# Load order, a second broadcast bank and a residual kept in DRAM in a two-layer mLSTM and attention trunk

## The chip, the cores and the metric

The kernel runs on one core of a Trainium2 chip. The metric is the device time of one execution in microseconds (us), as the median of several runs. One core has a matrix engine (PE), which multiplies, a vector engine (DVE), an activation engine (ACT), GpSimd (POOL) and a sync engine (SP), which here issues nearly all transfers between DRAM and the on-chip memory. Each engine takes its instructions strictly in the order of the program and meets the others through semaphores.

## The reference, cut to what matters

```python
def rmsnorm(x, g):
    return x * lax.rsqrt(jnp.mean(x * x, axis=-1, keepdims=True) + EPS) * g

def swiglu(h, w_gate, w_up, w_down):
    return (jax.nn.silu(h @ w_gate) * (h @ w_up)) @ w_down

h = x                                       # (1, 1024, 1024) float32, d_ff = 2816
for l in range(2):
    if l == 1:
        kv = rmsnorm(h, kv_norm_g) @ w_kv   # shared keys and values, 16 heads of 64
    hn = rmsnorm(h, norm_mix_g[l])
    if l == 0:
        h = h + mlstm_mixer(hn, ...)        # 8 heads, chunks of 64
    else:
        h = h + chunked_relpos_attention(hn, w_q, rel_table, w_o, k_sh, v_sh)
    h = h + swiglu(rmsnorm(h, norm_ffn_g[l]), w_gate[l], w_up[l], w_down[l])
return rmsnorm(h, final_norm_g)
```

## The kernel before, in words

All activations lie transposed: eight tiles of 128 features by 1024 tokens. A float32 product is made of three products of a short float type: ACT casts an operand to its high half (L174, L177, L965), DVE or GpSimd subtracts to get the low half (L175, L178, L967), and PE runs high times high, low times high and high times low. PE can start on an operand when its high half is there, and needs the low half one matmul later.

Both feed-forward blocks use seven block products in place of eight, with sums of blocks on either side. The gate and up projections, `gate_up`, go through 22 units of weight columns, n = 0 to 21, each with seven products, c = 0 to 6, of 12 matmuls into the PSUM tiles `a`, `b`, `c`, `d` (L989). `prepare(n, c)` makes the weight operand `wc` of product (n, c); units 0 and 1 run interleaved, since their first four products need only the left half of the tokens. During these first products the norm's scale is finished: `finish_a` sums squares over the features on PE (`f_ps`), DVE works out the inverse root (`f_y`), and `finish_b` spreads it with PE over all partitions into a PSUM bank (`f_pb`, four matmuls for each half of the tokens), from which ACT copies it to `f_rbc` (L341). Both halves use the same bank in turn.

The down projection, `down`, runs products i = 0 to 6 (operands b11, b21, t4, t3, t2, n1, b22, kept in DRAM by `gate_up`), each for u = 0 to 3, with 33 matmuls a product (PE line L1261, 11 blocks of the hidden features times three). `fetch(i, k)` loads block k of operand i into a tile of the `hr` pool (six tiles, 256 KB each) and splits it into `hc`; `wload(u, i, j)` loads a block of down weights (`wd`, 704 KB); `prepare(i, u)` splits such a block into `wc`, for which there are two tiles. For i = 0 the weights are loaded a second time, into three tiles of the `hr` pool (`wd1first`, L1157). The kept rows of the residual, `h[e]` (`hr` from `hd`, 512 KB), are loaded at L1238 and L1247, and DVE adds each product to them in `settle` (L1200); ACT copies the product of i = 0 to `v` (L1198).

At the end of layer 0 each row of the result is split into `xb{e}` high and low (`final`). The attention layer uses these halves, and at its end `out_a` puts the residual together again as high plus low with GpSimd (L1467). At that place PE runs the last attention products and the first half of the output projection (`oa_p`), whose operands `os0` to `os3` DVE splits (L175).

The final norm: `scale_out` sums squares over features on PE (`fin_ps`), works out the root on DVE (`fin_v` to `fin_y`), spreads it (`fin_pb`), and multiplies the rows on DVE (L1187) and GpSimd (L1185) before they are stored. It is called for the left half of the tokens after product (4, 3), and for two quarters after (6, 3, 0) and (6, 3, 1); in the last layer product 6 runs as two passes of 256 tokens.

SP issues all loads of these parts in one order. There are eight semaphores for its transfers, taken in turn, so an issue also waits for the eighth one before it to land.

Of the kernel before, what the change touches and what calls it, by code (L numbers as in the profile page):

```python
# [8 lines left out]
F32 = mybir.dt.float32  # L9
# [6 lines left out]
P = 128  # L16
T = 1024
# [23 lines left out]
def tile_trunk(  # L41
# [54 lines left out]
    def mxt(name):  # L96
        return pools["mx"].tile([P, HT], F32, tag="mx", name=name)
# [82 lines left out]
    def split(src, name, scale=None, pool="core"):  # L180
        hi = full(pool, f"{name}h", F32R)
        lo = full(pool, f"{name}l", F32R)
        split_into(hi, lo, src, scale)
        return hi, lo
# [103 lines left out]
    class Stats:  # L288
# [37 lines left out]
        def finish_b(self, r_tok, r_bc, cols=slice(0, T), pin=False):  # L326
            t0, nt = cols.start // P, (cols.stop - cols.start) // P
            for i0 in range(0, nt, 4):
                n = min(4, nt - i0)
                pb = mxt(f"{self.name}_pb{t0 + i0}")  # L330
                for i in range(n):
                    mm = nc.tensor.matmul(  # L332
                        pb[:, i * P : (i + 1) * P],
                        r_tok[:, i0 + i : i0 + i + 1].to_broadcast([P, P]),
                        ident,
                        start=True,
                        stop=True,
                    )
                    if pin:
                        tc.keep_in_program_order(mm)  # L340
                nc.scalar.copy(r_bc[:, (t0 + i0) * P : (t0 + i0 + n) * P], pb[:, 0 : n * P])  # L341
# [579 lines left out]
    def gate_up(layer, mixed, st):  # L921
# [24 lines left out]
        def prepare(n, c):  # L946

            if c == 0:
                load(n)
                load(n + 1)  # L950
            a11, a12, a21, a22 = (raws[n][:, i] for i in range(4))
            if c == (0 if n > 1 else 1):
                s1, s3 = swt(n, "s1"), swt(n, "s3")
                nc.vector.tensor_tensor(s1, a21, a22, ALU.add)
                nc.gpsimd.tensor_tensor(s3, a11, a21, ALU.subtract)
                sums[n] = [s1, None, s3, None]
            if c == 1:
                s2, s4 = swt(n, "s2"), swt(n, "s4")
                nc.vector.tensor_tensor(s2, sums[n][0], a11, ALU.subtract)
                nc.gpsimd.tensor_tensor(s4, s2, a12, ALU.subtract)  # L960
                sums[n][1], sums[n][3] = s2, s4
            s1, s2, s3, s4 = sums.get(n, [None] * 4)
            src = (a11, s2, s3, s1, a12, a22, s4)[c]
            t = full("hl", f"wc{layer}{n}_{c}", F32R)
            hi = nc.scalar.copy(t[:, 0:HT], src)  # L965
            eng = nc.gpsimd if n == 0 or (n, c) == (1, 0) else nc.vector
            eng.tensor_tensor(t[:, HT:T], src, t[:, 0:HT], ALU.subtract)  # L967
            ready[n, c] = t
            return hi
# [138 lines left out]
    def down(layer, mixed, hid):  # L1108
# [42 lines left out]
        def prepare(i, u, at=0):  # L1151
            t = pools["wc"].tile([P, 2, WC], F32R, tag="wc", name=f"wc{layer}{i}{u}{at}")
            block = ((0, 0), (0, 1), (1, 1), (1, 0), (1, 0), (0, 0), (0, 1))[i]
            for c, n in pieces:
                if i == 0:
                    src = hrt(f"wd{layer}first{u}{c}")[:, 0:n]
                    nc.sync.dma_start(src, wsrc(u, 0, 0)[:, c : c + n])  # L1157
                else:
                    src = raw[(u, *block)][:, c : c + n]
                split_into(t[:, 0, c : c + n], t[:, 1, c : c + n], src)  # L1160
            wcs[i, u, at] = t
# [10 lines left out]
        def final(e, i):  # L1172
            for cols in (hs(0),) if i == 0 else tails:
                st.add(h[e][:, cols], cols)
            if not last and i == 1:
                xs[e] = split(h[e], f"xb{e}")

        def scale_out(cols):
            r = r_fin[0]
# [48 lines left out]
        order = [(i, u, 0) for i in range(len(names)) for u in range(NU)]  # L1228
        if last:
            order += [(i, u, 1) for i, u, _ in order[-NU:]]  # L1230
        need = [("w", 0, 0, 0)] + [("x", 0, k) for k in range(NP)] + [("w", 0, 1, 0)]
        for step in need:
            (prepare if step[0] == "w" else fetch)(*step[1:])
        for e in range(NK):
            ht = coret(f"hr{layer}_{e}")
            h.append(ht)
        for u in range(NU):
            nc.sync.dma_start(h[u], mixed.kept[u])  # L1238
            wload(u, 0, 1)
        for m, (i, u, at) in enumerate(order):  # L1240
            if m + 2 < len(order) and order[m + 2][2] == 0:
                combine(*order[m + 2][:2])
            if m + 1 < len(order) and order[m + 1] not in wcs:
                prepare(*order[m + 1])
            if i == 0:
                wload(u, 0, 0)
                nc.sync.dma_start(h[u + NU], mixed.kept[u + NU])  # L1247
            if i == 0 and u >= 2:
                for v_ in (2 * u - 4, 2 * u - 3):
                    wload(v_, 1, 1)  # L1250
            if i == 2:
                wload(u, 1, 0)
            w = wcs.pop((i, u, at))
            n = HT // 2 if last and i == 6 else HT
            ps = pjt(f"dn{layer}{i}{u}{at}")[:, 0:n]
            for k in range(NP):
                wh, wl = (w[:, j, k * P : (k + 1) * P] for j in range(2))
                x = sums[i, k]
                xh, xl = (x[:, c + at * n : c + at * n + n] for c in (0, HT))
                for j, (a, b) in enumerate(((wh, xh), (wl, xh), (wh, xl))):  # L1260
                    nc.tensor.matmul(  # L1261
                        ps, a, b, start=(k == 0 and j == 0), stop=(k == NP - 1 and j == 2)
                    )
            if i + 1 < len(names):
                for k in (range(0, 2), range(2, 4), range(4, 5), range(5, NP))[u]:
                    fetch(i + 1, k)
            if i == 4:
                wload(u, 0, 1)
            settle(i, u, at, n, ps)
            if last and u == NU - 1:  # L1270
                if i == 4:
                    r_fin.append(coret("fin_rbc"))
                    scale_out(hs(0))
                if i == 6:
                    scale_out(slice(HT + at * n, HT + at * n + n))
        sb.close()
        return xs, st

    def ffn(layer, mixed, st):
        psc = Scope(mx=1, pj=7)  # L1280
        kept = gate_up(layer, mixed, st)
        psc.close()
        psc = Scope(mx=2, pj=6)
        res = down(layer, mixed, kept)
        psc.close()
        return res


    def attention(xs, st):
# [174 lines left out]
        def out_a():  # L1464
            for e in range(NK):
                ht = coret(f"h3_{e}")
                nc.gpsimd.tensor_tensor(ht, xs[e][0], xs[e][1], ALU.add)  # L1467
                hn.append(ht)
            osx = [split(ots[t], f"os{t}") for t in range(KB)]
            for e in range(NK):  # L1470
# [150 lines left out]
```

## Time and profile before

| what | value |
|---|---|
| runs | 2440.40, 2446.05, 2451.39 us (median 2446.05) |
| profiled execution | 2446.85 us, span from first to last instruction 2445.1 us |
| PE busy | 2332.5 us (95% of the span) |
| DVE busy | 1706.7 us (70%) |
| POOL busy | 1029.2 us (42%) |
| ACT busy | 975.9 us (40%) |
| PE clock, mean | 0.981 of full speed |

PE is busy for 95% of the span, so time can come from three places: the 112.6 us in which PE does nothing, stretches in which its granted clock is 0.5 of full speed (1.2 in place of 2.4 GHz), and the number of matmuls itself, which is the same in both kernels.

### The profile page before, as it was taken

Reading aid. Unit: us, or ns where it says so; the run is one execution under the profiler, and the core shown is the slowest. Engines: PE = TensorE matmul, PEld = TensorE weight load, DVE = VectorE, ACT = ScalarE, POOL = GpSimd, SP = SyncE. Lnnn points to the kernel's source line nnn. Section 1 sums busy time; section 2 is a strip of 40 time slices with the busy share of each in tenths; the row PEclk is TensorE's granted clock in tenths of the full one; section 3 lists DMA queues with packets and bytes.
Section 4 is the critical chain, followed back from the end, with each engine's and each line's share of the span. In section 5 each row is a group of like instructions: output and inputs, shape, how many; then the busy total and the mean of one; then the engine's idle time right before and its main releaser. Section 6 shows DMA issues by size and latency. Waiting matters only on the chain. (4 is left out here: it accounts for less than half of the span.)

```text
span 2445.1 us, 31222 instructions
## 1 busy us (share of the span) xinstructions
PE 2332.5 (95%) x11568; PEld 1929.3 (79%) x11568; DVE 1706.7 (70%) x2699; ACT 975.9 (40%) x1826; POOL 1029.2 (42%) x644
## 2 busy tenths in 40 slices
PE   8999999989999997999999999989889999997997
PEld 7888787777888886888878787868677888876877
DVE  6544455887777765797377777787887777764887
ACT  5322222442332323544366666655533322333444
POOL 2000000476666661122664545350776666640142
PEclk9999999989999998999999999999999999998999
DMA  3110102312223227542111111001312232239431
GB/s 135 44 35 26 44 19 86 131 67 104 101 94 116 100 103 291 205 142 76 53 45 39 37 38 40 32 23 45 122 70 98 96 129 91 104 124 355 159 124 52
DMA packets 91017, 232.00 MB, mean 95 GB/s; under 512 B 10096, under 2 KB 13424, under 8 KB 90864
## 3 DMA queue, kind: packets, MB, share of 16 engines
q1 hardware_dynamic: 89136, 227.91, 26.9%
q8 instruction: 90, 1.47, 0.3%
q10 hardware_dynamic: 1728, 2.10, 0.2%
q14 instruction: 63, 0.52, 0.1%
HBM read 177.01 MB, written 52.95 MB: 94 GB/s over the span
## 5 line engine op out<-in xcount | busy, mean ns | idle before, releaser
L1261 PE MATMUL dn<-hc,wc 128*128 128x512 f32 (+1 forms) x1980 | 432.7, 380 | 27.3 <-ACT wc L174 23.9
L1261 PEld LDWEIGHTS dn<-hc,wc 128*128 128x128 f32 x1980 | 357.0, 190 | 101.8 <-ACT wc L174 24.7
L989 PE MATMUL a<-b,wc 128*128 128x512 f32 x1056 | 261.6, 398 | 8.2 <-POOL wc L967 4.2
L989 PE MATMUL c<-t,wc 128*128 128x512 f32 x1056 | 257.6, 393 | 6.2 <-DVE c L1062 6.2
L989 PEld LDWEIGHTS a<-b,wc 128*128 128x128 f32 x1056 | 201.9, 191 | 55.0 <-ACT wc L965 4.9
L989 PEld LDWEIGHTS c<-t,wc 128*128 128x128 f32 x1056 | 199.2, 189 | 51.1 <-DVE c L1062 7.5
L967 DVE TENSOR_TENSOR wc<-s,wc 128x512 fp32r<-128x512 f32 x168 | 181.4, 1081 | 68.5 <-ACT wc L965 67.3
L965 ACT CAST wc<-s 128x512 fp32r<-128x512 f32 x176 | 107.7, 619 | 183.6 <-PE d L989 111.6
L730 POOL TENSOR_TENSOR hv<-num 128x1024 f32<-128x1024 f32 x8 | 15.2, 1895 | 342.4 <-ACT num L706 342.4
L174 ACT CAST wc<-wd 128x512 fp32r<-128x512 f32 x156 | 82.0, 582 | 141.4 <-PE dn L1261 132.0
L989 PE MATMUL b<-t,wc 128*128 128x512 f32 x528 | 131.6, 399 | 6.1 <-POOL wc L967 6.1
L175 DVE TENSOR_TENSOR hc<-hr,hc 128x512 fp32r<-128x512 f32 x154 | 105.3, 728 | 36.7 <-ACT hc L174 36.6
L989 PE MATMUL d<-b,wc 128*128 128x512 f32 x528 | 131.0, 397 | 0.0
L965 ACT CAST wc<-wr 128x512 fp32r<-128x512 f32 x132 | 80.5, 618 | 125.7 <-PE c L989 42.6
L989 PE MATMUL d<-n,wc 128*128 128x512 f32 x528 | 130.6, 396 | 0.0
L967 DVE TENSOR_TENSOR wc<-wr,wc 128x512 fp32r<-128x512 f32 x124 | 113.0, 912 | 20.0 <-ACT wc L965 20.0
L1400 ACT ACTIVATE p<-p,mn 128x640 f32<-128x640 f32 (+4 forms) x128 | 89.2, 697 | 87.8 <-DVE mn L1389 80.9
L989 PEld LDWEIGHTS b<-t,wc 128*128 128x128 f32 x528 | 100.7, 191 | 29.1 <-POOL wc L967 7.0
L174 ACT CAST hc<-hr 128x512 fp32r<-128x512 f32 x154 | 89.4, 617 | 72.4 <-DMA hr<-kb 53.2
L989 PEld LDWEIGHTS d<-b,wc 128*128 128x128 f32 x528 | 99.3, 188 | 24.1
L989 PEld LDWEIGHTS d<-n,wc 128*128 128x128 f32 x528 | 100.2, 191 | 21.7
L1022 POOL TENSOR_TENSOR c<-c,c 128x512 f32<-128x512 f32 x44 | 73.1, 1662 | 104.2 <-DVE c L1066 89.9
(817 smaller groups left out, 5828.2 us busy)
## 6 DMA issues: line engine op xcount, KB each, us to landing
wd<-in_w_down_dram SPq DMA_DIRECT2D x40, 704.0 KB, 7.8
wr<-in_w_gate_dram SPq DMA_DIRECT2D x44, 512.0 KB, 4.4
wr<-in_w_up_dram SPq DMA_DIRECT2D x44, 512.0 KB, 4.3
kb<-c SPq DMA_DIRECT2D x66, 256.0 KB, 2.3
kt<-t SPq DMA_DIRECT2D x66, 256.0 KB, 2.0
hr<-kb SPq DMA_DIRECT2D x66, 256.0 KB, 4.0
hr<-kt SPq DMA_DIRECT2D x66, 256.0 KB, 3.9
hd<-h SPq DMA_DIRECT2D x16, 512.0 KB, 2.7
```

Of the source, the lines that this page charges most:

```text
L174: nc.scalar.copy(hi, src)
L175: nc.vector.tensor_tensor(lo, src, hi, ALU.subtract)
L730: nc.gpsimd.tensor_tensor(x, nv, nv, ALU.mult)
L965: hi = nc.scalar.copy(t[:, 0:HT], src)
L967: eng.tensor_tensor(t[:, HT:T], src, t[:, 0:HT], ALU.subtract)
L989: nc.tensor.matmul(ps, a, b, start=(first and k == 0 and i == 0), stop=(k == len(xs) - 1 and i == 2), skip_group_check=True,)
L1022: nc.gpsimd.tensor_tensor(x, x, g, ALU.mult)
L1261: nc.tensor.matmul(ps, a, b, start=(k == 0 and j == 0), stop=(k == NP - 1 and j == 2))
L1400: nc.scalar.activation(p, p, AF.Exp, bias=mnv, scale=-1.0, accum_out=sm)
```

## The change

Five edits. In `down`, the weights of u = 2 and 3 for i = 0 come from the `wd` tiles that are loaded anyway, and not through `wd1first`; the loads are issued in another order, the residual rows one for each product. In `finish_b` with `pin`, the second half of the broadcast has a bank of its own. In `prepare`, the low halves of unit 0's products c = 0 and 1 are made by DVE and not by GpSimd. The result of layer 0 is stored to DRAM (`hm`) and loaded back in `out_a`, in place of GpSimd's additions. `scale_out` for the left half is called after (5, 0), and for the first quarter after (6, 0, 1).

```diff
-                pb = mxt(f"{self.name}_pb{t0 + i0}")
+                pb = (pjt if pin and i0 else mxt)(f"{self.name}_pb{t0 + i0}")
...
-            eng = nc.gpsimd if n == 0 or (n, c) == (1, 0) else nc.vector
+            eng = nc.gpsimd if n == 0 and c > 1 or (n, c) == (1, 0) else nc.vector
...
-                if i == 0:
+                if i == 0 and u < 2:
                     src = hrt(f"wd{layer}first{u}{c}")[:, 0:n]
...
                 xs[e] = split(h[e], f"xb{e}")
+                resid[e] = dram.tile([P, T], F32, tag=f"hm{e}", name=f"hm{e}")
+                nc.sync.dma_start(resid[e], h[e])
...
-        need = [("w", 0, 0, 0)] + [("x", 0, k) for k in range(NP)] + [("w", 0, 1, 0)]
-        for step in need:
-            (prepare if step[0] == "w" else fetch)(*step[1:])
+        prepare(0, 0)
+        for k in range(NP):
+            fetch(0, k)
+        prepare(0, 1)
+        for u in (2, 3):
+            wload(u, 0, 0)
         for e in range(NK):
-            ht = coret(f"hr{layer}_{e}")
-            h.append(ht)
-        for u in range(NU):
-            nc.sync.dma_start(h[u], mixed.kept[u])
-            wload(u, 0, 1)
+            h.append(coret(f"hr{layer}_{e}"))
...
             if i == 0:
-                wload(u, 0, 0)
+                wload(u, 0, 1)
+                nc.sync.dma_start(h[u], mixed.kept[u])
+            if i == 1:
                 nc.sync.dma_start(h[u + NU], mixed.kept[u + NU])
-            if i == 0 and u >= 2:
-                for v_ in (2 * u - 4, 2 * u - 3):
-                    wload(v_, 1, 1)
+                wload(u, 1, 1)
+                if u >= 2:
+                    wload(u - 2, 0, 0)
...
-            if last and u == NU - 1:
-                if i == 4:
-                    r_fin.append(coret("fin_rbc"))
-                    scale_out(hs(0))
-                if i == 6:
-                    scale_out(slice(HT + at * n, HT + at * n + n))
+            if last and (i, u) == (5, 0):
+                r_fin.append(coret("fin_rbc"))
+                scale_out(hs(0))
+            if last and (i, u, at) in ((6, 0, 1), (6, NU - 1, 1)):
+                c = HT if u == 0 else HT + n
+                scale_out(slice(c, c + n))
...
-                nc.gpsimd.tensor_tensor(ht, xs[e][0], xs[e][1], ALU.add)
+                nc.sync.dma_start(ht, resid[e])
```

SP's order where `down` of layer 1 starts, behind the last stores of `gate_up`; the kernel before (`hr_0` to `hr_4` from `hd` are residual rows, `hr_0` and `hr_1` from `kb` are operand blocks of i = 1, `wd` from 19267 on are the blocks for i = 1 and then i = 5):

```order
L1013 DMA kt_110_19148<-t_10_19137 128x512
L1238 DMA hr_1_19259<-hd_15467 128x1024
L1238 DMA hr_2_19260<-hd_15570 128x1024
L1128 DMA wd_19267<-in_w_down_dram 128x1408
L1128 DMA wd_19270<-in_w_down_dram 128x1408
L1128 DMA wd_19273<-in_w_down_dram 128x1408
L1238 DMA hr_3_19261<-hd_15754 128x1024
L1128 DMA wd_19276<-in_w_down_dram 128x1408
L1128 DMA wd_19278<-in_w_down_dram 128x1408
L1247 DMA hr_4_19262<-hd_15889 128x1024
L1134 DMA hr_0_19315<-kb_10_16144 128x512
L1157 DMA wd1first_19329<-in_w_down_dram 128x512
```

The kernel after the change, from the same store on (`wd_19262` and `wd_19264` are the blocks of u = 2 and 3 for i = 0):

```order
L1013 DMA kt_110_19152<-t_10_19141 128x512
L1134 DMA hr_0_19311<-kb_10_16148 128x512
L1134 DMA hr_2_19368<-kb_12_16754 128x512
L1128 DMA wd_19262<-in_w_down_dram 128x1408
L1128 DMA wd_19264<-in_w_down_dram 128x1408
L1128 DMA wd_19274<-in_w_down_dram 128x1408
L1128 DMA wd_19331<-in_w_down_dram 128x1408
L1248 DMA hr_1_19267<-hd_15471 128x1024
L1128 DMA wd_19388<-in_w_down_dram 128x1408
L1248 DMA hr_2_19268<-hd_15574 128x1024
L1128 DMA wd_19440<-in_w_down_dram 128x1408
L1248 DMA hr_3_19269<-hd_15758 128x1024
```

The weights of u = 2 now stand behind three operand blocks, where they stood behind five weight blocks, four residual rows and two operand blocks; the residual rows 1 to 3 stand behind four, five and six weight blocks.

DVE's order in the same stretch, the kernel before (`wc_19328` is the operand of u = 2, `wc_19391` that of u = 3, `wc_19453` that of i = 1, u = 0):

```order
L1200 TENSOR_TENSOR hr_0_19258<-hr_0_19258,dn_19281 128x512
L1200 TENSOR_TENSOR hr_1_19259<-hr_1_19259,dn_19344 128x512
L175 TENSOR_TENSOR hc_1_19322<-hr_1_19320,hc_1_19322 128x512
L175 TENSOR_TENSOR wc_19328<-wd1first_19329,wc_19328 128x512
L175 TENSOR_TENSOR hc_3_19385<-hr_3_19383,hc_3_19385 128x512
L175 TENSOR_TENSOR wc_19391<-wd1first_19392,wc_19391 128x512
L1200 TENSOR_TENSOR hr_2_19260<-hr_2_19260,dn_19411 128x512
L175 TENSOR_TENSOR wc_19453<-wd_19267,wc_19453 128x512 x2
```

The kernel after (`wc_19324` is u = 2, `wc_19381` u = 3, `wc_19433` i = 1, u = 0):

```order
L1202 TENSOR_TENSOR hr_0_19266<-hr_0_19266,dn_19277 128x512
L175 TENSOR_TENSOR hc_1_19318<-hr_1_19316,hc_1_19318 128x512
L175 TENSOR_TENSOR wc_19324<-wd_19262,wc_19324 128x512 x2
L175 TENSOR_TENSOR wc_19381<-wd_19264,wc_19381 128x512 x2
L1202 TENSOR_TENSOR hr_1_19267<-hr_1_19267,dn_19334 128x512
L175 TENSOR_TENSOR hc_3_19375<-hr_3_19373,hc_3_19375 128x512
L175 TENSOR_TENSOR wc_19433<-wd_19274,wc_19433 128x512 x2
L1202 TENSOR_TENSOR hr_2_19268<-hr_2_19268,dn_19391 128x512
L175 TENSOR_TENSOR hc_5_19479<-hr_5_19477,hc_5_19479 128x512
L1202 TENSOR_TENSOR hr_3_19269<-hr_3_19269,dn_19443 128x512
```

The splits of u = 2 and 3 moved ahead of the addition of residual row 1; row 1's addition now stands ahead of operand block 3 and of the first operand of i = 1, and row 3's ahead of operand blocks 6 to 10.

PE's order at the end of the first four products of `gate_up` in layer 0, the kernel before (`d_4172` and `d_4217` are the fourth products of units 0 and 1, `a_3975` is the fifth of unit 0):

```order
L989 MATMUL d_4172<-n_03_3972,wc_3_4108 128x512 x3
L332 MATMUL f_pb_4202<-packed,f_y 128x128 x4
L989 MATMUL d_4217<-n_01_3733,wc_3_4111 128x512 x3
L989 MATMUL d_4217<-n_02_3836,wc_3_4111 128x512
L332 MATMUL f_pb_4208<-packed,f_y 128x128 x4
L989 MATMUL d_4217<-n_02_3836,wc_3_4111 128x512 x2
L989 MATMUL d_4217<-n_03_3972,wc_3_4111 128x512 x3
L989 MATMUL a_3975<-b_00_4098,wc_4_4142 128x512 x3
```

The kernel after:

```order
L989 MATMUL d_4172<-n_03_3972,wc_3_4108 128x512 x3
L332 MATMUL f_pb_4202<-packed,f_y 128x128 x4
L332 MATMUL f_pb_4208<-packed,f_y 128x128 x4
L989 MATMUL d_4217<-n_01_3733,wc_3_4111 128x512 x3
L989 MATMUL d_4217<-n_02_3836,wc_3_4111 128x512 x3
L989 MATMUL d_4217<-n_03_3972,wc_3_4111 128x512 x3
L989 MATMUL a_3975<-b_00_4098,wc_4_4142 128x512 x3
```

Both broadcasts now run back to back, and the whole of `d_4217` follows them.

## Rows read from the trace of the kernel before

**Rows 1.** The page, part 1: busy time of each engine, share of the span, instructions.

```profile
PE 2332.5 (95%) x11568; PEld 1929.3 (79%) x11568; DVE 1706.7 (70%) x2699; ACT 975.9 (40%) x1826; POOL 1029.2 (42%) x644
```

**Rows 2.** PE's waits over the whole span: what waited, for what, us in total, times, longest.

```profile
PE dn L1261 <- ACT wc L174: 23.9, 2, 12.3
PE f_pb L332 <- ACT f_rbc L341: 10.6, 2, 5.3
...
PE c L989 <- DVE c L1062: 6.2, 3, 2.9
PE b L989 <- POOL wc L967: 6.1, 2, 3.4
PE a L989 <- POOL wc L967: 4.2, 2, 2.1
...
PE fin_ps L316 <- DVE fin_s L309: 3.4, 3, 1.7
...
PE fin_pb L332 <- DVE fin_y L285: 3.1, 2, 2.5
```

**Rows 3.** Windows at the start of `down` in layer 0 (first row) and layer 1: window, length, busy time of PE, PEld, DVE, ACT, POOL with instructions, granted PE clock, share of the DMA engines, GB/s. The windows of layer 1 end with the ACT copies of the products u = 0, 1, 2 and 3 of i = 0, that of layer 0 with u = 2.

```profile
953.00:974.40 21.40, 10.11 (x35) 7.86 (x36) 7.08 (x11) 6.21 (x12) 0.00 (x0) 0.68 1.03 406
...
2203.00:2210.40 7.40, 7.39 (x33) 5.72 (x31) 0.71 (x2) 0.51 (x1) 0.00 (x0) 1.00 1.03 383
2210.40:2233.30 22.90, 10.58 (x34) 8.22 (x35) 7.01 (x11) 6.37 (x12) 0.00 (x0) 0.70 1.03 406
2233.30:2240.90 7.60, 7.60 (x35) 6.22 (x34) 2.36 (x4) 2.08 (x5) 0.00 (x0) 1.00 1.02 413
```

**Rows 4.** The chain that ended last, in order of time, from 2195 to 2245 us: start, length, what.

```profile
2203.31 8.86 DMA wd<-in_w_down_dram
...
2212.23 9.74 DMA wd1first<-in_w_down_dram
...
2222.05 0.63 ACT wc L174
```

**Rows 5.** SP's queue in the same stretch, in order of time: start, length of the issuing, line, tiles, count.

```profile
2199.67 2.08 SPq L1013 DMA_DIRECT2D kt<-t  x2
2201.84 0.88 SPq L1238 DMA_DIRECT2D hr<-hd  x2
2202.77 1.40 SPq L1128 DMA_DIRECT2D wd<-in_w_down_dram  x3
...
2212.23 3.35 SPq L1157 DMA_DIRECT2D wd1first<-in_w_down_dram  x3
```

**Rows 6.** Windows at the start of `gate_up` in layer 0; columns as in rows 3.

```profile
515.00:530.00 15.00, 9.72 (x44) 8.09 (x43) 15.00 (x16) 7.95 (x13) 9.10 (x6) 0.77 0.08 31
530.00:545.00 15.00, 15.00 (x66) 12.23 (x66) 13.99 (x13) 4.99 (x9) 14.18 (x10) 1.00 0.24 88
```

**Rows 7.** The same stretch in order of time, on ACT, DVE and POOL: start, length, engine, line, operation, tiles.

```profile
524.27 0.56 ACT L341 COPY f_rbc<-f_pb 128x512 f32<-128x512 f32 x1
...
518.78 1.77 DVE L954 TENSOR_TENSOR s<-wr 128x512 f32<-128x512 f32 x1
...
527.26 0.74 DVE L178 SCALAR_TENSOR_TENSOR b<-h,packed,b 128x512 fp32r<-128x512 f32 x1
527.92 1.77 DVE L959 TENSOR_TENSOR s<-s,wr 128x512 f32<-128x512 f32 x1
...
529.11 1.75 POOL L1004 TENSOR_TENSOR c<-c,f_rbc 128x512 f32<-128x512 f32 x1
```

**Rows 8.** Line L967, the low half of `wc`, on DVE and on POOL: count, shortest, median and longest duration in ns.

```profile
L967 DVE TENSOR_TENSOR wc<-wr,wc x124: 672/692/1778, 510.6 to 2164.2; 128x512 fp32r<-128x512 f32 x124
...
L967 POOL TENSOR_TENSOR wc<-wr,wc x8: 1287/1504/1726, 487.3 to 1764.9; 128x512 fp32r<-128x512 f32 x8
```

**Rows 9.** The end of the attention layer: two windows (columns as in rows 3), then instructions on DVE and POOL in order of time.

```profile
1604.00:1631.00 27.00, 17.72 (x84) 13.39 (x82) 24.55 (x38) 15.55 (x30) 21.70 (x10) 0.94 0.07 22
1624.00:1627.50 3.50, 3.26 (x9) 2.78 (x10) 3.46 (x10) 0.66 (x3) 1.31 (x1) 0.51 0.03 12
...
1614.04 2.56 DVE L175 TENSOR_TENSOR os0l<-ot,os0h 128x1024 fp32r<-128x1024 f32 x1 [0.76 <-ACT os0h L174]
...
1619.10 0.28 DVE L1389 CUSTOM_DVE_ANT_0 p<-s,bias 128x128 f32<-128x128 f32 x1
...
1619.31 2.66 DVE L162 TENSOR_TENSOR wl_oa<-wr_oa,wh_oa 128x512 fp32r<-128x512 f32 x1
1621.89 2.28 DVE L175 TENSOR_TENSOR os1l<-ot,os1h 128x1024 fp32r<-128x1024 f32 x1
...
1625.32 1.21 DVE L175 TENSOR_TENSOR os2l<-ot,os2h 128x1024 fp32r<-128x1024 f32 x1
...
1618.78 2.64 POOL L1467 TENSOR_TENSOR h<-xb7h,xb7l 128x1024 f32<-128x1024 f32 x1
```

**Rows 10.** The final norm of the left half, on PE and DVE in order of time.

```profile
2367.26 1.02 PE L316 MATMUL fin_ps<-ones,fin_s 128*128 128x1 f32 x8 [1.70 <-DVE fin_s L309]
2368.15 4.13 PE L1261 MATMUL dn<-hc,wc 128*128 128x512 f32 x10
...
2383.50 2.80 PE L1261 MATMUL dn<-hc,wc 128*128 128x512 f32 x11 [1.17 <-DVE wc L175]
...
2373.82 6.63 DVE L1187 SCALAR_TENSOR_TENSOR hr<-hr,packed,fin_rbc 128x512 f32<-128x512 f32 x5 [2.34 <-ACT fin_rbc L341]
```

More of the change, by code (lines that the diff above doesn't have):

```diff
@@ L1286, in ffn @@
         return res
+    resid = {}
     def attention(xs, st):
```

## The prediction

> **What bounds the kernel now.** The first view is the page's busy times: PE works 2332.5 of 2445.1 us [rows 1], and both kernels run the same matmuls, so only the 112.6 us in which PE stands, and the stretches at half clock, can change. The next view is the list of PE's waits. Its top is `dn` waiting for the cast of `wc`, 23.9 us in essentially two waits, one a layer; then come the broadcast `f_pb`, 10.6 us in two waits, and the small waits for low halves from POOL [rows 2]. Other engines matter only where they end last ahead of a PE wait, so each edit is costed at its own place, first by windows, then by the order of time there.
>
> The long wait is read from the chain at the start of `down`. Product u = 1 of i = 0 ends at 2210.40; the loads of `wd1first` for u = 2 are only issued at 2212.23 and take 9.74 us, behind earlier `wd` loads of 8.86 us [rows 4], of which SP had put three into the queue from 2202.77 on [rows 5]. The DMA engines are full there: share 1.03 at 383 to 413 GB/s [rows 3]. So the weights that PE needs next stand behind blocks that it needs two products later or more.
>
> **The change part by part.**
>
> *Down start.* An undisturbed product takes 7.40 to 7.60 us, say 7.5; u = 2 takes 22.90 us in layer 1 and 21.40 in layer 0 [rows 3]. That is 15.4 + 13.9 = 29.3 us lost, 24 of it idle and the rest at the clock: the granted mean in these windows is 0.70 and 0.68, between the two levels of 1.2 and 2.4 GHz.
> After the change, only three operand blocks (0.79 MB) lie between the last store and the 0.72 MB of u = 2's weights. The stores end their issue at 2201.75 [rows 5]; with some 2 us for the store to land (estimated from the chain's and queue's pace), 1.51 MB at 383 GB/s takes 3.9 us: landing at 2207.7 at best, and about 2209.5 if stores and operands share the pipe with it to the end. Cast (0.63, [rows 4]) and low half (0.7, [rows 8]) follow, so PE finds it ready between 2209.0 and 2210.8, and wants it at 2210.4. I take 0.5 us left over per layer, giving **28.3 us**.
> What is late next: between that store and the last operand block of i = 1 the new queue holds 11 operand blocks (2.88 MB), six weight blocks (4.33 MB) and three residual rows (1.57 MB), 8.8 MB. At the measured 406 GB/s [rows 3] they take 21.6 us and end near 2225.5 to 2227. i = 1 starts at 2210.4 + 2 × 7.5 = 2225.4 and wants block 5 after five elevenths of a product, 2228.8, block 10 at 2232.2. DVE has the additions of rows 1, 2 and 3 ahead of these splits, in order: each can hold up everything behind it. By the same sum row 1 lands some 11 us after the store (4.2 MB at 406), near 2215, while its product ended at 2210.4, so DVE stands there, but what is queued behind (first operand of i = 1) is wanted only at 2225.4. The slack at block 10 is about 1.5 us with splits of 0.7 each. So I keep the 28.3; the other bound is half of it returned in i = 1, 14 us.
> A page speaks against this: the Trainium skill, "SBUF — State Buffer", section "Summary: rules for kernel authors", would plan transfers from DRAM at about 358 GB/s. The rows show 406 and 413 GB/s, so the trace disagrees; by the page's rate the same 8.8 MB would take 24.6 us, end near 2229 and cost each layer some 2 us, a total of about 2408.
>
> *Second bank and unit 0's low halves.* The `f_pb` wait of 5.3 us a layer goes [rows 2], because PE no longer needs ACT's copy at 524.27 [rows 7] before the second broadcast. But the product after it needs the low half of the last `b` block, which DVE makes at 527.26 [rows 7], and DVE is busy all 15.00 of 15 us there [rows 6]. The change moves one sum of 1.77 us (L954, 518.78) and one low half of 0.69 behind it, so that block comes some 2.5 us earlier, and PE, there sooner, stands again. From 528 on POOL works 14.18 and DVE 13.99 of 15 us [rows 6]; POOL's chain of gate products starts with L1004 at 529.11 [rows 7], and in the new order the sum of 1.7 us that POOL had done early now stands just ahead of it. So POOL can start that chain 1.7 us earlier at most, and the wait of `c` for DVE (6.2 us over both layers, [rows 2]) at its end takes the rest. Low halves of c = 0 and 1 cost 0.69 on DVE in place of 1.50 us on POOL [rows 8] and shorten two waits (4.2 and 6.1 us, [rows 2]), in time that DVE's chain mostly claims back. I take 1.6 us a layer, **3.2 us**. Bounds: 0, if both chains give all back; 6 a layer, if the shift is carried through, 12.
>
> *Residual through DRAM.* The last GpSimd addition, 2.64 us at 1618.78, and seven before it go. In 1604 to 1631 PE is busy 17.72 of 27 us; 1.6 more are lost at a granted 0.51 [rows 9]. DVE, at 24.55 of 27, bounds it: two splits beside GpSimd's additions take 2.56 and 2.28 us, the same split after them 1.21; a weight split takes 2.66, where the same kind of subtraction has a median of 0.69 [rows 8, 9]. These three give back 4.4 us. I take 4.9 of the 9.3 idle and the 1.6 of clock, **6.5 us**; bounds 0 and 10.
> The loads cost SP and DMA 4.2 MB at 406 GB/s, 10.3 us, beside 22 GB/s of other traffic [rows 9]. They start as the query products release the tiles; the seven unbroken GpSimd additions that wait for the same halves began near 1603 (1618.78 less six of 2.6 us), so the loads end between 1614 and 1620. The residual itself is wanted after 1630, but SP's next load behind it is the bias of the last head pair, which DVE reads at 1619.10 [rows 9]: no cover to spare. A late bias holds the weight split and `os1l` behind it on DVE one for one, up to some 4 us, which is inside the bounds. The stores run beside the last products of `down` in layer 0, whose weights are all loaded by then: **0**; without that cover they would cost the same 10.3 us.
>
> *Final norm.* The first call moves behind (5, 0), so its sum is ready when PE gets there: the waits of 1.70 and 1.17 us go, and ten matmuls take 4.13 us where 33 take 7.40, thus 1.9 us of half clock [rows 3, 10]; the quarter's 0.6 us (3.1 less 2.5, [rows 2]) goes too. Of these 5.4 I keep **4.5 us**: the five multiplications of 6.63 us on DVE now stand ahead of the split for the product after next, ready just about when PE wants it. Bounds 2 and 5.4. The last quarter's tail is unchanged.
>
> *Sum.* 28.3 + 3.2 + 6.5 + 4.5 = 42.5. The profiled execution took 2446.85 us, 0.8 over the median of the runs: 2446.85 - 42.5 = 2404.3, say **2404 us**.
>
> **The rivals.**
> (A) *The loads are still late in part.* DMA stays full, and DVE, held by residual rows 1 to 3, makes blocks 5 to 10 of i = 1 late. For it: share 1.03 now; against it: 21.6 us of transfers in 22 to 28 us of room. Half lost: 2418; all lost, as if the edit did nothing: 2432.6.
> (B) *Only the down start and the final norm pay.* DVE and POOL take back everything in `gate_up`, and a late bias everything in attention: 2446.85 - 32.8 = 2414. For it: DVE at 15.00 of 15 and 24.55 of 27 [rows 6, 9].
> (C) *The gate-up shift is carried through*: 12 in place of 3.2, thus 2395; with 10 in attention 2392. For it: POOL has 5.9 us free in 515 to 530; against it: 14.18 of 15 behind [rows 6].
> (D) *The transfers run slower than 406 GB/s.* At 383, the lowest of these windows [rows 3], 8.8 MB take 1.4 us longer, which uses up the slack at block 10 and costs up to 1 us a layer: 2406. The 358 of the page named above gives its 2408.
> (E) *Slower:* the additions of rows 1, 2, 3 and the splits of operand blocks stand in one order on DVE, and each late load stops all of them. If in both layers each of four such loads came one product (7.5 us) after it is wanted, 60 us would be lost, 2464; it decides against the change from 42.5 / 8 = 5.3 us a load on. By the sums above they come 1.5 to 10 us before they are wanted.
>
> **How the numbers follow.** Forecast 0.50 (2398 to 2411), D 0.05, A 0.17 (half of it at 2432), B 0.14, C 0.11, E 0.02, no change 0.01. The range runs from C with its bounds, 2391, to A's half with attention's loss, 2424; it leaves out about 0.1 above and 0.05 below. A measurement here tells 0.5% (12 us) from no change: faster means below 2434. That holds for all but E, no change and a little of A: faster 0.93, same 0.05, slower 0.02.
>
> **What would show it.** Right: the `dn` wait for the cast falls from 23.9 to under 2 us, and both windows of u = 2 take 7.5 to 8; no `f_pb` wait, but a new one of 2 to 4 us for DVE's `b` just behind, and a `c` wait no smaller; `os0l` and `os1l` near 1.2 us; PE's half clock after the final norm gone. Wrong: new waits of `dn` in i = 1 for `hc` (A, D or E), a wait of `s` or `p` for the bias near 1619, or gate-up ending over 5 us sooner (C).

## The result, and the profile after

The changed kernel takes 2408.3 us (median of four runs, 2406.05 to 2409.20) against 2445.8 us for the kernel before, measured beside it: a ratio of 0.9845, with a 95% interval of 0.9822 to 0.9868. It is faster by 37.5 us, 1.5%. The forecast was 2404 us, in a range of 2391 to 2424. The profiled execution took 2409.20 us with a span of 2407.2. The runs below come from several chips, each with its own runs of the kernel before, whose medians lie between 2445.8 and 2447.5 us; each ratio is to these.

The page after answers to [rows 1]; matmuls and their number are the same, and the part of the span in which PE does nothing fell from 112.6 to 78.9 us:

```profile
PE 2328.3 (97%) x11568; PEld 1928.0 (80%) x11568; DVE 1708.5 (71%) x2703; ACT 974.3 (40%) x1826; POOL 986.4 (41%) x632
```

PE's waits after (waiting line, releaser, us in total, times, longest) answer to [rows 2]:

```profile
PE c L989 <- DVE c L1062: 17.1, 2, 9.6
PE b L989 <- DVE wc L967: 7.0, 2, 3.5
...
PE a L989 <- ACT wc L965: 4.1, 2, 2.1
...
PE dn L1264 <- DVE wc L175: 2.8, 4, 1.2
PE fin_ps L316 <- DVE fin_s L309: 2.7, 2, 1.5
...
PE oa_p L204 <- DVE os0l L175: 0.7, 1, 0.7
```

The waits of 23.9 us for the cast of `wc` and of 10.6 us of `f_pb` are gone. The `c` wait grew from 6.2 to 17.1 us, and `b` waits 7.0 in place of 6.1, for VectorE where it had waited for GpSimd. In the two gate-up stages together PE is idle as long as before: 26.7 us (900.50 less 873.81) against 27.2. The sums over both stages, first the kernel before, then the changed one:

```profile
sum 899.50, PE 872.32 PEld 711.21 DVE 669.38 ACT 292.19 POOL 590.45; mean PE 436.16 PEld 355.60 DVE 334.69 ACT 146.10 POOL 295.22
```

```profile
sum 900.50, PE 873.81 PEld 713.13 DVE 674.55 ACT 292.44 POOL 585.43; mean PE 436.90 PEld 356.57 DVE 337.28 ACT 146.22 POOL 292.71
```

The stages of all kernels are compared in one table. It is worked out from each profiled execution: gate-up of a layer runs from its first matmul of L989 to the first `dn` matmul, down 0 from the first to the last `dn` of layer 0, attention from there to layer 1's first L989, and the last column from layer 1's first `dn` to the end. The part ahead of the first L989 is not in the table; no edit lies in it, and it took 483.4 to 487.1 us. The text of a stage that two kernels share gave 449.2 to 450.5 us in gate-up, 568.5 to 573.2 in attention and 234.3 to 236.5 in the last column, so a smaller difference between two single executions is not clear of noise. The labels are explained under the experiments.

| kernel | median us | gate-up 0 | down 0 | attention | gate-up 1 | down 1 to the end |
|---|---|---|---|---|---|---|
| before | 2445.8 | 449.6 | 226.7 | 580.9 | 450.0 | 251.4 |
| changed | 2408.3 | 450.3 | 213.5 | 570.6 | 450.2 | 235.9 |
| loads_only | 2419.8 | 450.4 | 213.9 | 580.2 | 449.9 | 236.7 |
| twice | 2404.7 | 450.4 | 212.9 | 572.6 | 450.5 | 234.7 |
| pool_adds | 2419.6 | 449.7 | 212.8 | 584.9 | 450.2 | 235.8 |
| pool_adds_own | 2414.8 | 450.2 | 214.2 | 575.8 | 450.2 | 235.9 |
| no_gate | 2406.0 | 449.6 | 213.1 | 570.8 | 450.3 | 235.8 |
| no_bank | 2405.6 | 449.0 | 213.8 | 568.5 | 448.9 | 235.5 |
| no_low | 2408.1 | 451.5 | 213.1 | 571.4 | 451.4 | 236.5 |
| fin51 | 2408.0 | 449.2 | 212.7 | 572.3 | 449.8 | 237.9 |
| defer | 2401.2 | 446.7 | 213.2 | 571.2 | 447.0 | 234.5 |
| nogate_defer | 2399.8 | 446.0 | 213.5 | 571.9 | 446.6 | 234.3 |
| best | 2400.2 | 446.2 | 212.9 | 572.9 | 446.4 | 234.4 |
| best_fin51 | 2399.6 | 445.2 | 216.6 | 573.2 | 446.4 | 236.4 |

The windows of the down start after (columns as in [rows 3]) end, as there, with ACT's copies of the products of i = 0; the rows are u = 1 of layer 0, u = 2 of layer 0, u = 1 and u = 2 of layer 1:

```profile
946.26:954.51 8.25, 8.03 (x35) 6.05 (x33) 2.99 (x6) 3.29 (x6) 0.00 (x0) 1.00 1.00 359
954.51:962.08 7.57, 7.57 (x33) 6.25 (x34) 4.70 (x8) 3.17 (x7) 0.00 (x0) 1.00 1.02 411
...
2180.53:2188.92 8.39, 8.04 (x35) 6.05 (x33) 2.99 (x6) 3.29 (x6) 0.00 (x0) 1.00 1.01 371
2188.92:2196.51 7.59, 7.59 (x33) 6.25 (x34) 4.71 (x8) 3.18 (x7) 0.00 (x0) 1.00 1.02 415
```

The windows of u = 2 take 7.57 and 7.59 us in place of 21.40 and 22.90, at full clock. They flatter u = 2 a little: in layer 1 its first matmul came at 2188.14, but ACT was casting weights and copied the product of u = 1 only at 2188.92, so that the window of u = 1 is too long by what the next one is too short. Both products together take 15.98 us in layer 1, where they took 30.30. The DMA engines are as full as before (1.02); the bytes that are wanted first now come first.

### The profile page after: what moved, and what is told of

The parts are those of the page before. It is cut to its first block, busy times and chain, and to the rows that moved or that the text cites. A ratio compares the mean times of both kernels' runs of the same rounds, so it can differ in the third digit from the quotient of the medians.

```text
span 2407.2 us, 31213 instructions
## 1 busy us (share of the span) xinstructions
PE 2328.3 (97%) x11568; PEld 1928.0 (80%) x11568; DVE 1708.5 (71%) x2703; ACT 974.3 (40%) x1826; POOL 986.4 (41%) x632
## 5 line engine op out<-in xcount | busy, mean ns | idle before, releaser
L989 PE MATMUL c<-t,wc 128*128 128x512 f32 x1056 | 260.0, 396 | 17.1 <-DVE c L1062 17.1
L989 PE MATMUL a<-b,wc 128*128 128x512 f32 x1056 | 260.1, 396 | 6.7 <-ACT wc L965 4.1
L989 PEld LDWEIGHTS c<-t,wc 128*128 128x128 f32 x1056 | 201.1, 191 | 62.2 <-DVE c L1062 17.9
L989 PEld LDWEIGHTS a<-b,wc 128*128 128x128 f32 x1056 | 200.7, 190 | 53.0 <-ACT wc L965 5.0
L967 DVE TENSOR_TENSOR wc<-s,wc 128x512 fp32r<-128x512 f32 x170 | 187.1, 1102 | 68.5 <-ACT wc L965 67.3
L174 ACT CAST wc<-wd 128x512 fp32r<-128x512 f32 x168 | 89.0, 581 | 149.4 <-PE dn L1264 120.5
L989 PE MATMUL b<-t,wc 128*128 128x512 f32 x528 | 134.9, 406 | 7.0 <-DVE wc L967 7.0
L989 PE MATMUL d<-b,wc 128*128 128x512 f32 x528 | 131.4, 398 | 0.0
L989 PE MATMUL d<-n,wc 128*128 128x512 f32 x528 | 128.2, 392 | 0.0
L967 DVE TENSOR_TENSOR wc<-wr,wc 128x512 fp32r<-128x512 f32 x126 | 117.0, 929 | 15.1 <-ACT wc L965 15.1
L989 PEld LDWEIGHTS b<-t,wc 128*128 128x128 f32 x528 | 103.1, 196 | 30.6 <-DVE wc L967 7.8
L175 DVE TENSOR_TENSOR wc<-wd,wc 128x512 fp32r<-128x512 f32 x168 | 120.1, 754 | 10.7 <-ACT wc L174 10.4
L989 PEld LDWEIGHTS d<-b,wc 128*128 128x128 f32 x528 | 99.8, 189 | 24.3
L989 PEld LDWEIGHTS d<-n,wc 128*128 128x128 f32 x528 | 99.0, 188 | 21.5
```

Source lines behind the costliest of these rows:

```text
L174: nc.scalar.copy(hi, src)
L175: nc.vector.tensor_tensor(lo, src, hi, ALU.subtract)
L989: nc.tensor.matmul(ps, a, b, start=(first and k == 0 and i == 0), stop=(k == len(xs) - 1 and i == 2), skip_group_check=True,)
```

## The experiments

**loads_only: the largest edit alone.** The kernel before with the load order and the single loads of the change; the other four edits undone.

> The kernel before with the new load order and single loads in the down projection alone; the other four edits undone. Theory (the edits add up by place): the two down starts gain 13.3 and 14.4 us as in the changed kernel's trace, so 2445.8 - 27.7 = about 2418 us, and nothing else in the trace moves by more than 1 us. Rival (part of the gain came from another edit, or the loads alone cost something later): outside 2414 to 2422.

2419.8 us; ratio to the kernel before 0.9878 (0.9855 to 0.9901). Down 0 falls by 12.8 us, the last column by 14.7; the other stages stay. So this edit by itself carries 27.5 us by stages, 26.5 by the medians (2446.2 before, on that chip), of the 37.5.

**twice: order against second load.** The changed kernel's order, with the weights of u = 2 and 3 loaded a second time as before.

```diff
-                if i == 0 and u < 2:
+                if i == 0:
...
-        for u in (2, 3):
-            wload(u, 0, 0)
...
-                if u >= 2:
-                    wload(u - 2, 0, 0)
+                wload(u, 0, 0)
```

> The changed kernel with the weights of u = 2 and 3 for i = 0 loaded a second time into the hr tiles as before (1.44 MB more in each layer), but in the new order. Theory (the order of the loads is the cause, the second load costs its 3.5 us of transfers against 1 to 2 us of room): no wait of 10 us for u = 2, waits of 0 to 3 us a layer in i = 0 or i = 1: 2408 to 2415 us. Rival (the second load and its place in the hr tiles is the cause): a wait near 10 us in each layer, 2425 us or more.

2404.7 us, 0.9827 (0.9802 to 0.9852): no slower than the changed kernel. PE's order of time at the same place shows one unbroken piece:

```profile
2184.74 12.52 PE L1261 MATMUL dn<-hc,wc 128*128 128x512 f32 x54
```

The 1.44 MB more in each layer cost nothing that shows: down 0 and the last column are 212.9 and 234.7 us, within the spread of the changed kernel's. The order of the loads was the cause of the down starts' gain, and the theory's 3.5 us for the second load was wrong.

**pool_adds and pool_adds_own: why the attention layer gained more.** Sixteen GpSimd additions that nobody needs are put back at the old place. In pool_adds their result goes to the pool of half tiles:

```diff
                 nc.sync.dma_start(ht, resid[e])
+                vv = vt[KB * 2 - 1].rearrange("p a b c -> p (a b c)")
+                pa = halft(f"pa{e}")
+                for j in range(2):
+                    nc.gpsimd.tensor_tensor(pa, vv[:, hs(j)], vv[:, hs(j + 2)], ALU.add)
```

> The changed kernel with sixteen GpSimd additions of 128x512 put back at the place of the removed ones, on data that nobody waits for and whose result nobody reads. Theory (contention: VectorE's instructions stretch while GpSimd reads SBUF): os0l and os1l take 2.2 to 2.6 us again in place of 1.2, and the end of the attention layer loses 5 to 10 of its 10.1 us: 2413 to 2418 us. Rival (the gain came from the release of the old additions' tiles, for which ScalarE's os0h waited, and not from contention): within 2 us of 2408.

2419.6 us, attention 584.9 in place of 570.6: more than the whole gain, and above what its theory expected. But VectorE's waits there show a cost of the experiment itself, tiles of that pool for which `pl` waited:

```profile
DVE pl L1439 <- POOL pa L1476: 5.3, 2, 2.9
```

So pool_adds_own writes into a tile of the values that is out of use; its additions read the loaded rows (`hn`, two the first and fourteen the last one), which sets when they can start.

```diff
+            vv = vt[KB * 2 - 1].rearrange("p a b c -> p (a b c)")
+            pa = vt[KB * 2 - 3].rearrange("p a b c -> p (a b c)")
+            for j in range(16):
+                nc.gpsimd.tensor_tensor(
+                    pa[:, hs(j % 2)], hn[0 if j < 2 else 7][:, hs(j % 2)], vv[:, hs(j % 2)], ALU.add
+                )
             osx = [split(ots[t], f"os{t}") for t in range(KB)]
```

> As pool_adds, but the sixteen additions write into a tile of the values that is out of use, so that no tile of VectorE's pl waits for GpSimd (in pool_adds VectorE stood 5.3 us for that). Theory (contention): os0l to os3l stretch to 1.8 to 2.6 us as in pool_adds, the attention layer takes 5 to 10 us more than the changed kernel's 570.6, 2413 to 2418 us. Rival (pool_adds was slow by its own tile waits, the removed additions cost little by contention): within 2 us of 2408.

2414.8 us, 0.9865 (0.9849 to 0.9882): 6.5 over the changed kernel's median, 5.2 in the attention stage, where its 575.8 lie 2.6 us above the longest of the ten kernels with the changed text. The order of time on VectorE and GpSimd (start, length, line, tiles), first pool_adds_own, then the changed kernel, then the kernel before:

```profile
1587.05 1.98 DVE L175 TENSOR_TENSOR os4l<-ot,os4h 128x1024 fp32r<-128x1024 f32 x1
...
1599.31 2.03 DVE L175 TENSOR_TENSOR os0l<-ot,os0h 128x1024 fp32r<-128x1024 f32 x1
1604.00 2.32 DVE L175 TENSOR_TENSOR os1l<-ot,os1h 128x1024 fp32r<-128x1024 f32 x1
1606.45 2.11 DVE L175 TENSOR_TENSOR os2l<-ot,os2h 128x1024 fp32r<-128x1024 f32 x1
...
1602.57 21.98 POOL L1477 TENSOR_TENSOR vb<-h,vb 128x512 fp32r<-128x512 f32 x14
```

```profile
1598.69 2.08 DVE L175 TENSOR_TENSOR os0l<-ot,os0h 128x1024 fp32r<-128x1024 f32 x1
1602.38 1.21 DVE L175 TENSOR_TENSOR os1l<-ot,os1h 128x1024 fp32r<-128x1024 f32 x1
1603.72 1.21 DVE L175 TENSOR_TENSOR os2l<-ot,os2h 128x1024 fp32r<-128x1024 f32 x1
```

```profile
1599.92 1.98 DVE L175 TENSOR_TENSOR os4l<-ot,os4h 128x1024 fp32r<-128x1024 f32 x1
...
1603.13 2.51 POOL L1467 TENSOR_TENSOR h<-xb1h,xb1l 128x1024 f32<-128x1024 f32 x1
...
1621.39 1.71 POOL L1362 TENSOR_TENSOR ql<-qs,qh 64x512 fp32r<-64x512 f32 x1
```

`os1l` and `os2l` stretch from 1.21 to 2.32 and 2.11 us when GpSimd adds beside them, and PE waits 2.6 us for `os1l`, where it waits 0.4 in the changed kernel. So GpSimd additions beside VectorE's splits are shown to cost this stage about 5 us, half of the 10.3 by which attention shrank. That the old additions cost just that is not shown, since they stood elsewhere: counted from `os4l`, they ran unbroken from 3.2 us on in the kernel before, the fourteen only from 15.5 us on. They also held GpSimd's next pair of query splits back to 1621.39, behind the last addition, where the changed kernel has that pair ahead of `os1l`, from 1598.39 on; and ScalarE's `os0h`, for which `os0l` waited 0.76 us, came late. These parts are not separated. (`os0l` is long in both, since GpSimd's query splits run beside it.)

**no_gate, no_bank, no_low: the start of gate-up.** Both edits there undone, then one at a time.

```diff
-                pb = (pjt if pin and i0 else mxt)(f"{self.name}_pb{t0 + i0}")
+                pb = mxt(f"{self.name}_pb{t0 + i0}")
...
-            eng = nc.gpsimd if n == 0 and c > 1 or (n, c) == (1, 0) else nc.vector
+            eng = nc.gpsimd if n == 0 or (n, c) == (1, 0) else nc.vector
```

The first pair of lines is no_bank, the second no_low, both are no_gate.

> The changed kernel with both edits of the gate-up start undone (one broadcast bank; GpSimd makes unit 0's low halves of c = 0 and 1). Theory, after the trace: both edits together bring nothing there, since the wait of product c for VectorE grows by what the broadcast wait loses (layer 0 reaches the down start 0.8 us later, layer 1 0.2 us later): 2408 -1 +/- 2, about 2407 us. Rival, the forecast's 3.2 us gain, hidden in this profiled execution by something else: about 2411.5 us.

2406.0 us, 0.9826 (0.9804 to 0.9847); gate-up 449.6 and 450.3, as in the changed kernel. The two edits together bring nothing that can be measured.

> The changed kernel with one broadcast bank again; VectorE still makes unit 0's low halves of c = 0 and 1. Theory (neither edit of the gate-up start is worth anything by itself, since VectorE's and GpSimd's chain behind decides when c is free): f_pb waits some 10 us again, the c wait shrinks from 17 to about 6 us, 2406 to 2410 us. Rival (the bank gains, the low halves cost by the longer b wait of 3.5 us and the half clock behind it): about 2411 us.

> The changed kernel with unit 0's low halves of c = 0 and 1 back on GpSimd; two broadcast banks. Same theory: the a wait is 2.1 us a layer again, b 2.7 to 3.5, the c wait near 15 us, 2406 to 2410 us. Rival (the low halves on VectorE cost, the bank gains): about 2404 us.

2405.6 us (0.9832, 0.9808 to 0.9857) and 2408.1 us (0.9841, 0.9813 to 0.9869). Their medians lie too near each other to part the edits, but gate-up does in both layers: 449.0 and 448.9 with the low halves alone, 451.5 and 451.4 with the bank alone, some 2.5 us a layer between them, in one execution each. The rival had it the wrong way round: by these stages the second bank is what costs a little, the low halves on VectorE gain a little. The waits of PE, first no_bank, then no_low:

```profile
PE f_pb L332 <- ACT f_rbc L341: 10.5, 2, 5.9
PE c L989 <- DVE c L1062: 7.5, 3, 3.6
```

```profile
PE c L989 <- DVE c L1062: 8.1, 2, 4.2
...
PE a L989 <- DVE b L178: 5.3, 2, 2.7
```

With the bank, the wait of `f_pb` (10.8 us in no_gate) turns into 5.3 us for VectorE's last `b` block and a longer `c` wait (8.1 us, 5.9 in no_gate), as forecast; the expectation for no_low had that `c` wait near 15 us. With the low halves too, `b` is in time and the whole wait moves to `c` (17.1 us).

**defer: what holds `c`.** The four block sums at the end of the first pair of units moved behind unit 2's fourth product (they are collected in a list at n = 1 and run there).

```diff
+            if p == 0:
+                tails_.append(tail)
+            else:
+                tail()
...
             done(p + NP, 1, c22)
+            while n == 2 and tails_:
+                tails_.pop()()
             yield
```

> The changed kernel with the four block sums at the end of the first pair of gate-up units (n1, t2, t3, t4 of pair 0) moved behind the fourth product of unit 2. Theory (the c wait of 7.5 and 9.6 us is VectorE's order: the sums, which wait for GpSimd, stand ahead of the addition that frees c): the wait ends 3 to 4 us earlier in each layer, with less half clock behind it: 2408 - 7 to -12, about 2398 us. Rival (GpSimd's chain of gate products decides, the order on VectorE does not): wait unchanged, 2406 to 2410 us.

2401.2 us, 0.9808 (0.9791 to 0.9826): 7.1 us below the changed kernel. Gate-up falls by 3.6 and 3.2 us, clear of the spread, and the `c` wait from 17.1 to 10.1:

```profile
PE c L989 <- DVE c L1071: 10.1, 2, 6.1
```

On VectorE in layer 0, first changed, then defer:

```profile
556.63 0.69 DVE L1033 TENSOR_TENSOR n<-c,v 128x512 f32<-128x512 f32 x1 [1.15 <-POOL v L1022]
557.36 1.63 DVE L1035 TENSOR_TENSOR t<-c,n 128x512 f32<-128x512 f32 x1
558.91 1.75 DVE L967 TENSOR_TENSOR wc<-s,wc 128x512 fp32r<-128x512 f32 x1
...
562.25 0.68 DVE L1062 TENSOR_TENSOR c<-c,v 128x512 f32<-128x512 f32 x1
```

```profile
554.67 2.35 DVE L967 TENSOR_TENSOR wc<-s,wc 128x512 fp32r<-128x512 f32 x2
556.94 0.68 DVE L1066 TENSOR_TENSOR v<-b,cp 128x512 f32<-128x512 f32 x1
...
558.61 0.68 DVE L1071 TENSOR_TENSOR c<-c,v 128x512 f32<-128x512 f32 x1
```

The addition that frees `c` needs nothing from the sums that stood ahead of it; it came at 562.25 and comes at 558.61. So 7.0 of the 17.1 us of the `c` wait were that order. The rest is left; in this trace three weight splits stand ahead of the same addition without a gap, but moving them was not tried.

**nogate_defer, best, best_fin51: is there a faster version.**

> The changed kernel with both gate-up edits undone and the four block sums of pair 0 moved behind the fourth product of unit 2. Theory (the addition that frees c then comes 3 to 4 us earlier, and the broadcast wait lets PE arrive later): the c wait of 3 us a layer is gone, with its half clock: 2406 - 6 to -10, about 2398 us, no slower than with the gate-up edits kept (2401). Rival (with the edits kept PE gains more once c comes earlier): 2403 us or more.

> The changed kernel with one broadcast bank, the block sums of pair 0 moved behind unit 2's fourth product, and the weights of u = 2 and 3 loaded a second time in the new order. Theory (stages add up): gate-up 450.3 to about 446 us in each layer (-8.5 in all), the down starts another 1.5: 2408 - 10, about 2398 us, below both kernels. Rival (the moved sums already take all that the bank edit lost): 2400 to 2402 us.

2399.8 us (0.9813, 0.9788 to 0.9838) and 2400.2 us (0.9810, 0.9797 to 0.9824): no clear difference from defer's 2401.2. So with the sums moved, neither gate-up edit matters, and the parts do not add up as the theory for best had it: moving the sums already takes what the others could give. By their medians all three are below both kernels of the case; the intervals of their ratios touch that of the changed kernel, but gate-up at 446 to 447 us against 450 lies clear of the spread.

**fin51: the final norm one product later.** One line, `(5, 0)` replaced by `(5, 1)`.

> The changed kernel with the left half's final norm called one product later, after (5, 1). Theory (the sum of squares still passes VectorE and ScalarE in order behind two weight splits and ends 1.2 us after PE wants it, and half clock follows): one product later the sum has been there for 6 us, the fin_ps wait of 1.23 us and its 1.7 us of half clock are gone, the last stage shrinks from 235.9 to about 233.5: 2408 - 2 to -3, about 2405.5 us. Rival (the 6.6 us of multiplications on VectorE then meet a split that PE wants, and a new wait takes their place): 2407 us or more, with a dn wait of 1 to 3 us.

2408.0 us; the last column grows from 235.9 to 237.9. These 2.0 us are no more than the spread between executions, but they come again between best and best_fin51 (234.4 to 236.4). The rival was right. PE's order of time shows `fin_ps` without a wait, and the new wait for a split, behind the five multiplications that then run from 2345.46 for 6.62 us:

```profile
2337.42 0.95 PE L316 MATMUL fin_ps<-ones,fin_s 128*128 128x1 f32 x8
...
2362.10 4.22 PE L1264 MATMUL dn<-hc,wc 128*128 128x256 f32 x21 [1.30 <-DVE wc L175]
```

> The kernel named best with the left half's final norm called after (5, 1). Theory (as for that edit alone): another 2 to 3 us, about 2395.5 us. Rival: no change against it, 2398 us.

2399.6 us, 0.9812 (0.9796 to 0.9828), as best: again no gain. (Its profiled execution, at 2405.34 us, was the longest of its four.)

## Why the prediction was right, point by point

**Down start: right.** 28.3 us forecast; 27.5 by loads_only. The step "what is late next" held as told: the cast of u = 2's weights on ACT started at 2187.46, PE wanted it at 2188.00, and two small gaps (0.13 and 0.22 us) are all that is left. Row 1's addition came at 2193.90, 5.9 us after its product, and nobody waited for it; there is no `dn` wait in i = 1.

```profile
2187.46 1.55 ACT L174 CAST wc<-wd 128x512 fp32r<-128x512 f32 x3 [2.53 <-DMA wd<-in_w_down_dram]
```

```profile
2193.90 0.69 DVE L1202 TENSOR_TENSOR hr<-hr,dn 128x512 f32<-128x512 f32 x1 [1.48 <-DMA hr<-hd]
```

Rival A fell, and with it D and E: the 359 to 415 GB/s of the windows above were enough. That the total by D's slower rate, 2408, is nearest to the measured 2408.3 is chance: it rests on late blocks in i = 1, and none was late. What the forecast did not see is that the second load was free (twice).

**Second bank and low halves: the size was wrong.** Forecast 3.2 us, measured -0.9 (stage table), which is nothing within the spread, so rival B was right for this place. The step "POOL can start that chain 1.7 us earlier at most" was in order (527.99 in place of 529.11), but the step behind it, that a part of this start is carried through, was not. The sum L960 on GpSimd stood behind two of these gate products and stands ahead of them in the new order. There it waits 1.23 us for VectorE's half of the sum, and the chain that started 1.1 us sooner ends 1.0 us later (L1008). First the kernel before, then the changed one:

```profile
543.08 1.74 POOL L960 TENSOR_TENSOR s<-s,wr 128x512 f32<-128x512 f32 x1
...
546.82 1.30 POOL L1008 TENSOR_TENSOR v<-v,f_rbc 128x512 f32<-128x512 f32 x1 [0.74 <-ACT v L1007]
```

```profile
540.31 1.30 POOL L960 TENSOR_TENSOR s<-s,wr 128x512 f32<-128x512 f32 x1 [1.23 <-DVE s L959]
...
547.80 1.30 POOL L1008 TENSOR_TENSOR v<-v,f_rbc 128x512 f32<-128x512 f32 x1 [0.74 <-ACT v L1007]
```

The sign "a new wait of 2 to 4 us for DVE's `b` just behind" did not show in the changed kernel, only in no_low; the whole wait went to `c`, which the forecast had only as "no smaller". And the forecast left out the clock behind the waits. After the 3.50 us wait of `b` in layer 0 PE ran at a granted 0.50 for 13.6 us; in layer 1 such a stretch began within the `c` wait of 9.61 us and took in the 6.2 us of matmuls behind it:

```profile
498.40:512.00 13.60, 13.03 (x39) 10.95 (x40) 9.98 (x17) 5.78 (x11) 8.27 (x6) 0.50 0.17 58
...
1788.60:1802.30 13.70, 6.19 (x15) 4.84 (x16) 10.59 (x12) 2.28 (x4) 9.58 (x7) 0.50 0.42 154
```

**Residual through DRAM: the mechanism right in part, the size too small.** Forecast 6.5 us, measured 10.3 in the attention stage between the two profiled executions (7.0 to 12.4 if all kernels with the old and the changed text are compared). That contention of this kind can cost half of it is shown (pool_adds_own); how much of it the old additions cost is not. Two readings were off. Of the two long splits only `os0l` ran beside an addition: the last one ended at 1621.42, and `os1l` started at 1621.89, beside the query splits that the additions had held back. And the sign "`os0l` and `os1l` near 1.2 us" came true for `os1l` alone (1.21); `os0l` took 2.08. The step on the loads was too late in its times. SP issued the first at 1572.77 and the other seven from 1585.52 on, and the last landed by 1598.0. The changed kernel comes to this place some 13.5 us earlier (its `os4l` starts at 1586.36), so in the times of the kernel before that is from 1599 on, and landed by 1611.5, where the forecast had 1603 and 1614 to 1620.

```profile
1585.52 3.75 SPq L1472 DMA_DIRECT2D h<-hm  x7
...
1597.73 0.33 SPq L1377 DMA_DIRECT2D bias<-in_rel_dram  x1
```

The bias behind them was issued when its buffer came free, no later than that; it was not the one that VectorE reads first there (at 1598.47, before this one had landed), so the cover that the forecast missed existed.

**Final norm: the size was wrong.** Forecast 4.5 us; the last column is 0.8 shorter than in loads_only, which has the old places, and that is within the spread. "Its sum is ready when PE gets there" failed: the sum passes VectorE and ScalarE in order, behind an addition that takes 1.79 us while GpSimd adds too, and two weight splits, and ends 1.23 us late, and half clock followed as before. So of the 1.70 us of this wait 1.23 stayed, and the half clock behind it (forecast as 1.9 us of gain); the wait of 1.17 us for a split behind it is gone.

```profile
2329.05 1.79 DVE L1211 TENSOR_TENSOR hr<-hr,v 128x512 f32<-128x512 f32 x1
2330.76 2.25 DVE L175 TENSOR_TENSOR wc<-wd,wc 128x512 fp32r<-128x512 f32 x2
2332.94 0.68 DVE L309 TENSOR_TENSOR fin_s<-fin_s,fin_q 128x512 f32<-128x512 f32 x1
...
2333.67 1.05 PE L316 MATMUL fin_ps<-ones,fin_s 128*128 128x1 f32 x8 [1.23 <-DVE fin_s L309]
```

**The sum.** Forecast 28.3 + 3.2 + 6.5 + 4.5 = 42.5; by stages 27.5 - 0.9 + 10.3 + 0.8 = 37.7, against 37.9 us between the two spans. The down start, three quarters of the gain, was right in size and in mechanism. Of the other terms two were too large by 7.8 us together and one too small by 3.8, so that the total came within 5 us is in part luck.

## What to carry to other kernels

When transfers are saturated, first put them in the order in which their bytes are wanted: here 1.44 MB a layer loaded twice cost nothing that shows, and bytes that stood ahead of needed ones cost some 14 us a layer. A wait that is removed ahead of engines that are nearly fully busy may only move, as the 10.6 us of `f_pb` did here: look for the instruction that stands ahead of the next release without belonging to it, and move that. Waits that stay cost more than their length: here stretches of 3.4 to 13.7 us at half clock followed or began in them, so count PE's half-clock stretch with each.

## What the runs showed of the hardware

The half-clock stretch behind a wait differed at one and the same place: after `b` waits of 3.50 us in layer 0 and 3.46 us in layer 1 of the changed kernel, the granted clock was 0.50 for 13.6 us in the first case and for 3.4 us in the second.

```profile
1734.00:1737.40 3.40, 3.40 (x10) 2.63 (x9) 2.55 (x4) 3.26 (x7) 1.48 (x2) 0.50 0.00 0
1737.40:1751.00 13.60, 13.60 (x72) 11.56 (x71) 13.35 (x24) 5.52 (x10) 8.78 (x6) 1.00 0.44 154
```

Of fin51, whose program is the same there, the trace has a `b` wait of 2.36 us in layer 0 and full clock behind it:

```profile
495.00:512.00 17.00, 14.65 (x72) 12.37 (x73) 15.92 (x25) 7.20 (x14) 10.12 (x8) 1.00 0.24 80
```

By an estimate some 5 us of time can come or go in that way, with nothing changed in the program near it: half of the 13.0 less 3.4 us in which PE worked at a granted 0.50 in the two layers. What decides it was not tested. It is also not why the gate-up edits brought nothing, since fin51 took 449.2 us there without that stretch, 449.6 before.
